# Two sets' w_out_c products run beside the last pair's chain in phase 1 of a hybrid convolution and RWKV-7 step

## The chip, the cores and the metric

The kernel runs on one core of a Trainium2 chip. The metric is the device time of one execution in microseconds; it was timed in three runs, and one further execution was profiled. TensorE (PE) multiplies, with its weight loads counted apart (PEld), VectorE (DVE) and ScalarE (ACT) do the elementwise work, GpSimd (POOL) some of it, and SyncE (SP) issues nearly all DMAs from one queue, in order.

## The reference, cut to what matters

```python
def _layer(x, conv_buf, h_last, S0, norm_g, w_in, conv_w, ...):
    h = _rmsnorm(x, norm_g)
    p = jnp.einsum('bsd,dn->bsn', h, w_in)
    p_conv, p_rwkv, p_gate = _split(p, [N_CONV_COLS, N_RWKV_COLS, 2 * D_MODEL])
    xin, bg, cg, zc = _split(p_conv, CONV_SIZES)
    u = cg * xin
    ...
    y_c = bg * conv * jax.nn.silu(zc)
    ...
    S_fin, ys = _rwkv7_scan(S0, r_h, k_h, v_h, decay.reshape(hs), kk, a_h)
    ...
    y_r = ((yn + bonus) * jax.nn.silu(zr.astype(jnp.float32))).astype(x.dtype)
    gc, gr = _split(p_gate, [D_MODEL, D_MODEL])
    pc = jnp.einsum('bsc,cd->bsd', y_c, w_out_c)
    pr = jnp.einsum('bsc,cd->bsd', y_r, w_out_r)
    m = jax.nn.sigmoid(gc) * pc + jax.nn.sigmoid(gr) * pr
    out = jnp.einsum('bsd,de->bse', m, w_o)
    return x + out, new_conv, h[:, -1], S_fin.astype(S0.dtype)
```

The width D is 1024. The prompt has 2048 tokens; beside it 8 sequences of 4 tokens each continue from a stored state. A final RMSNorm closes the step. All is float32.

## The kernel before

**Sets, pairs, blocks.** The prompt is cut into 4 sets of 512 tokens; the last set (`LAST`) also carries the 32 tokens of the 8 sequences. A block is one projection of 128 output columns over a set: 8 input tiles, three float32r matmuls each (high weights by high input, low by high, high by low), so 24 matmuls of up to 512 columns (`proj`, into one of three PSUM banks called ip). Weights are split into high and low parts once (ACT copy, DVE subtraction, from wraw into whl, 4 buffers each), stored to a scratch in HBM, and loaded from there by the later sets.

**Phase 1.** The main stream runs all input projections, set by set, with the split input in XH and XL. The conv branch's result yc, the gates' tanh gc and gr, and the RWKV branch's result yr go to HBM. Beside the main stream run side jobs (`Side`), one chain of them for each of the 8 head pairs of a set, 32 in all, numbered 0 to 31: keys, solve, merge and load (`begin_pair`), then the chain over 8 chunks (`rwkv_chain`), the 8 sequences (`rwkv_sequences`, last set only) and the group norm with its output (`rwkv_out`), all three started by `run_pair`. A chain step is three small products that wait for each other through DVE and ACT: pa (state by AR), pb (us by the inverse Xbd), pb (SV by BKt, which gives the new state S). A side job gets a stretch of the main stream (`over`, from the fractions in `CUTS`; the unit is three matmuls of 512 columns, 8 to a block), and a clock model (`Clock`) decides between which matmuls each of its steps is put. The scheduler that builds the program moves a few more instructions. The last pair of the last set has 13 own blocks in the main stream; pair 30's chain, sequences and group norm run beside them. Pair 31's run after the main stream's end (`run_pair(*before, 8.0, True)`, `finish_sides`).

**Phase 3.** For each set in turn: a merge stage of 16 blocks (8 by w_out_c with yc in XH and XL, 8 by w_out_r with yr in RH and RL, in turn), where DVE and ACT evacuate with the gates (gt) into MH and ML; then an output stage, 192 matmuls with w_o (240 for the last set) into PSUM banks called po, the residual and the norm. `load_y` brings yc and yr of the next set in during the output stage. Phase 3's tiles take over the SBUF of phase 1's, so their first writers wait for the last users of that memory.

Names in the trace: all compute instructions are issued by one helper, line 117, and all SP DMAs by line 168 (121 and 172 in the changed kernel), so tiles tell the work: ip projections, po output products, pa and pb the chain, pt every other small product.

Of the kernel before, what the change touches and what calls it, by code (L numbers as in the profile page):

```python
# [16 lines left out]
P = 128  # L17
# [7 lines left out]
SIDES = {"first": 8.0, "late": 14.0, "keys": 30.0, "solve": 30.0, "merge": 8.0, "load": 8.0, "samp": 20.0, "out": 12.0, "prep": 10.0, "y": 4.0, "chain": 45.0, "zero": 1.0}  # L25
# [6 lines left out]
        "end": (0.4, 0.1, 0.4, 0.2, 0.4, 0.6, 0.6)}  # L32
WAHEAD = 4

BACKLOG, URGENT = 1800.0, ("chain", "merge", "load", "samp", "prep")
# [140 lines left out]
def hybrid_kernel(tc, x_prompt, x_sample, state_conv, state_shift, state_rwkv, norm_g, w_in, conv_w,  # L176
# [955 lines left out]
    def rwkv_sequences(th, p, o):  # L1132
# [4 lines left out]
        s0 = wraw_p.tile([64, NS, 2, 64], F32, name="wraw")  # L1137
# [106 lines left out]

    EDGE = 3
# [4 lines left out]
    for th in range(NSETS):  # L1250
        for p in range(NB):
# [9 lines left out]
            else:  # L1261
                plan.append((th, whole(bl), p, None))
# [15 lines left out]
    for th in range(NSETS):  # L1278
        for nm, b in MERGE:
            wsrc = w_out_c if nm == "c" else w_out_r  # L1280
            keep(("o" + nm, th, b), wsrc[0][:, b * P:(b + 1) * P])
# [3 lines left out]
    def main_stream(parts):  # L1285
        for x, c0, c1 in parts:
            need(*(job.get(("prep", x.key[1], hf)) for hf in range(2) if (c1 > HN if hf else c0 < HN)))
            yield from x.part(c0, c1)

    def load_y(th, nm):  # L1290
# [5 lines left out]
        def load(b, j):  # L1296
            raw = (wraw_p if th == 0 else o2).tile([P, 1024], F32, name="wraw" if th == 0 else "yraw")[:, 0:nt]
# [91 lines left out]
    for th, hv, p, nx in plan:  # L1389
# [11 lines left out]
        if nx is not None:  # L1401
            e = EDGE / 2 * NB
# [3 lines left out]
    run_pair(*before, 8.0, True)  # L1406
    Side(load_y(0, "c"), "y").over(0, 1)
# [128 lines left out]
```

## Time and profile before

| | |
|---|---|
| runs timed | 3239.68, 3247.93, 3248.16 us; median 3247.93 us |
| profiled execution | 3239.32 us, span 3237.6 us |
| PE busy | 3109.5 us (96%) |
| DVE, ACT, POOL busy | 1999.7 (62%), 1243.0 (38%), 308.7 us (10%) |
| mean granted TensorE clock | 0.987 |
| HBM read and written | 447.90 and 155.17 MB |
| chain that ended last | PE 67%, DVE 20%, ACT 5%, issue 5%, DMA 2% |

A busy engine is one with an instruction in it; TensorE's matmuls are pipelined, so the time of one is longer than the distance to the next. The chain that ended last is followed back from the last instruction to what released each step. Times in rows are from the span's start.

### The profile page before, as it was taken

What the parts mean: (1) busy time and instruction counts of PE and PEld (TensorE: products, weight loads), DVE (VectorE), ACT (ScalarE), POOL (GpSimd) and SP (SyncE); (2) the same over time, 40 slices, a digit from 0 to 9 for tenths busy, and PEclk for the clock granted to TensorE, in tenths of its full rate; (3) what the DMA queues carried; (4) which work ended last, traced back from release to release, by engine and by line L of the source; (5) the groups of instructions that cost most, each with busy time, mean ns of one, the idle gap of its engine ahead of it and who ended that gap; (6) DMA issues with size and microseconds to landing.
All of it is one profiled execution on the core that took longest, in us unless ns stands there. A gap on an engine that the chain in (4) does not pass through costs nothing.

```text
span 3237.6 us, 54951 instructions
## 1 busy us (share of the span) xinstructions
PE 3109.5 (96%) x21234; PEld 2585.9 (80%) x21234; DVE 1999.7 (62%) x5703; ACT 1243.0 (38%) x2580; POOL 308.7 (10%) x517
## 2 busy tenths in 40 slices
PE   7999999999999999999999999999999969999998
PEld 6777777877777778777777899888898847788897
DVE  5687777776666657666666676666777745433332
ACT  5454544444334443443433344443444422211201
POOL 2011111110000111110001010100100000000000
PEclk9999999999999999999999999999999979999999
DMA  7786667644444444444444444434433339988773
GB/s 265 256 269 210 223 221 222 213 158 143 152 161 157 157 155 173 155 159 149 158 157 157 145 159 140 133 135 136 139 130 132 122 126 320 351 307 312 265 257 119
DMA packets 233308, 606.66 MB, mean 187 GB/s; under 512 B 32906, under 2 KB 136451, under 8 KB 179286
## 3 DMA queue, kind: packets, MB, share of 16 engines
q1 hardware_dynamic: 232902, 602.61, 54.4%
q8 instruction: 168, 2.75, 0.3%
q14 instruction: 94, 0.77, 0.1%
q0 software_dynamic: 144, 0.52, 0.0%
HBM read 447.90 MB, written 155.17 MB: 186 GB/s over the span
## 4 chain that ended last, share of the span: by engine, by line
PE 67%; DVE 20%; ACT 5%; issue 5%; DMA 2%; POOL 1%; SPq 0%; ACTq 0%; DVEq 0%; POOLq 0%
PE ip L117 48%; PE pt L117 10%; PE po L117 6%; DVE X L117 3%; DVE tt L117 3%; PE pb L117 3%; DVE tmp L117 2%; ACT tmp L117 2%; DVE Mi L117 2%; DVE whl L117 1%; DVE us L117 1%; DVE S L117 1%; PE pa L117 1%; ACT Xbd L117 1%; DVE GM L117 1%
## 5 line engine op out<-in xcount | busy, mean ns | idle before, releaser
L117 PE MATMUL ip<-XH,whl 128*128 128x512 f32 (+3 forms) x7408 | 2053.4, 356 | 6.6 <-DVE whl L117 1.9
L117 PEld LDWEIGHTS ip<-XH,whl 128*128 128x128 f32 x7408 | 1287.3, 190 | 183.2 <-issue 28.4
L117 PE MATMUL ip<-XL,whl 128*128 128x512 f32 (+3 forms) x3704 | 1316.1, 355 | 2.6 <-POOL XL L117 2.6
L117 PEld LDWEIGHTS ip<-XL,whl 128*128 128x128 f32 x3704 | 702.6, 190 | 80.4 <-issue 6.2
L117 DVE TENSOR_TENSOR X<-X,tt 128x60 f32<-128x60 f32 (+24 forms) x992 | 211.4, 213 | 27.4
L117 DVE TENSOR_TENSOR tt<-Mi,X 128x60 f32<-128x60 f32 (+24 forms) x992 | 209.8, 212 | 28.0
L117 DVE SCALAR_TENSOR_TENSOR S<-pb,pe,sp 64x64 f32<-64x64 f32 x512 | 143.6, 281 | 101.7 <-PE pb L117 95.5
L117 ACT ACTIVATE sp<-S,pe 128x128 f32<-128x128 f32 x256 | 99.5, 399 | 258.2 <-DVE S L117 254.9
L117 ACT ACTIVATE tmp<-ip,vec 128x512 f32<-128x512 f32 (+2 forms) x174 | 103.1, 593 | 231.4 <-PE ip L117 230.0
L117 ACT COPY SV<-pb 64x64 f32<-64x64 f32 x256 | 53.3, 208 | 330.2 <-DVE SV L117 326.3
L117 PE MATMUL ip<-RH,whl 128*128 128x512 f32 (+2 forms) x640 | 170.3, 355 | 4.9 <-ACT RH L117 4.9
L117 PE MATMUL po<-whl,MH 128*128 128x512 f32 x544 | 170.7, 394 | 1.2 <-ACT whl L117 1.1
L117 DVE TENSOR_TENSOR whl<-wraw,whl 128x1024 fp32r<-128x1024 f32 x105 | 134.2, 1279 | 53.3 <-ACT whl L117 52.8
L117 DVE SCALAR_TENSOR_TENSOR gt<-gt,ip 128x512 f32<-128x512 f32 (+1 forms) x80 | 46.9, 586 | 169.3 <-PE ip L117 167.1
L117 DVE TENSOR_TENSOR us<-pa,P 64x64 f32<-64x64 f32 x512 | 110.1, 215 | 57.5 <-PE pa L117 38.4
L117 ACT CAST whl<-wraw 128x1024 fp32r<-128x1024 f32 x105 | 109.5, 1044 | 60.6 <-DMA wraw<-in_w_out_r_dram 25.5
L117 PEld LDWEIGHTS pb<-us,Xbd 128*128 128x128 f32 x512 | 86.4, 190 | 57.6 <-PE ip L117 19.7
L117 PEld LDWEIGHTS ip<-RH,whl 128*128 128x128 f32 x640 | 112.8, 189 | 23.7 <-issue 4.0
L117 PEld LDWEIGHTS pb<-SV,BKt 128*128 128x128 f32 x512 | 85.3, 190 | 57.4 <-ACT SV L117 48.7
L117 PE MATMUL pb<-SV,BKt 128*128 128x128 f32 x512 | 108.1, 293 | 18.6 <-ACT SV L117 18.2
L117 PEld LDWEIGHTS po<-whl,MH 128*128 128x128 f32 x544 | 102.1, 188 | 25.6 <-ACT whl L117 1.6
L117 DVE TENSOR_TENSOR GM<-pt,mask_p 128x512 f32<-128x512 f32 x128 | 82.4, 685 | 61.4 <-PE pt L117 61.4
(489 smaller groups left out, 3940.5 us busy)
## 6 DMA issues: line engine op xcount, KB each, us to landing
wraw<-in_w_in_dram SPq DMA_DIRECT2D x81, 512.0 KB
whl<-w_k SPq DMA_DIRECT2D x24, 1024.0 KB
whl<-w_r SPq DMA_DIRECT2D x24, 1024.0 KB
whl<-w_v SPq DMA_DIRECT2D x24, 1024.0 KB
whl<-w_z SPq DMA_DIRECT2D x24, 1024.0 KB
whl<-w_xin SPq DMA_DIRECT2D x24, 1024.0 KB
whl<-w_cg SPq DMA_DIRECT2D x24, 1024.0 KB
whl<-w_zc SPq DMA_DIRECT2D x24, 1024.0 KB
```

The source lines that it names most:

```text
L117: r = f(*a, **k)
```

## The change

The w_out_c blocks of sets 0 and 1 (`PRE`) are appended to the main stream of the last pair of phase 1, behind its 13 own blocks: 16 blocks, the first three and last three of each set in halves of 256 columns. Their input yc is loaded into the freed buffers of the even pairs (AR0, Xbd0, GM0) and split into XH and XL by half sets (`load_first`), when the last block that reads that half is through. `merge_first` loads gc, forms (gc + 1) times the product, and stores it over gc in HBM. At the end yr of set 1 is loaded the same way. Pair 31's chain, sequences and group norm get stretches of that longer main stream (`TAIL`), pair 30's jobs new fractions (`CUTS["end"]`, of a total that is 238.5 in place of 110.5 units). Phase 3 begins with set 1, whose w_out_r blocks (`merge_second`) read XH and XL, then takes set 0 with w_out_r blocks alone, then sets 2 and 3 as before. gt has 6 buffers in place of 4.

```diff
 CUTS = {"most": (0.7, 0.0, 0.0, 0.34, 0.7, 0.95, 0.95), "last": (0.6, 0.3, 0.68, 0.4, 0.7, 0.97, 0.9),
-        "end": (0.4, 0.1, 0.4, 0.2, 0.4, 0.6, 0.6)}
+        "end": (0.2,0.03,0.22,0.1,0.25,0.32,0.28)}
+
+TAIL = (0.32,0.52,0.32,0.52,0.65)
+PRE = (0, 1)
+FIRST = PRE[-1]
 WAHEAD = 4
...
-        s0 = wraw_p.tile([64, NS, 2, 64], F32, name="wraw")
+        if end_(th, p):
+            s0 = GMB[(th * NB + p + 1) % 2].rearrange("p a b c d -> p (a b c d)")[0:64, 0:NS * P].rearrange(
+                "v (j h k) -> v j h k", h=2, k=64)
+        else:
+            s0 = wraw_p.tile([64, NS, 2, 64], F32, name="wraw")
...
+    def merge_first(th, b):
+
+
+        def begin():
+            o["g"] = tmp.tile([P, TW], F32, name="tmp")
+            SP.dma_start(out=o["g"][:, 0:NT], in_=gc_d[th][b])
+        def evac(c0, c1, ps):
+            g = o["g"][:, c0:c1]
+            V.scalar_tensor_tensor(out=g, in0=g, scalar=1.0, in1=ps[:, 0:c1 - c0], op0=ALU.add, op1=ALU.mult)
+        def end():
+            SP.store(gc_d[th][b], o["g"][:, 0:NT])
+        return Block(("oc", th, b), w_out_c[0][:, b * P:(b + 1) * P], evac, begin, end)
...
+    def load_first(nm, th, hf):
+        cs = slice(hf * HN, (hf + 1) * HN)
+        raws = []
+        for q in range(NB // KG):
+            raws.append(ring[len(turn) % len(ring)])
+            turn.append(q)
+            for i in range(KG // 2):
+                SP.dma_start(out=raws[q][:, 2 * i:2 * i + 2, :],
+                             in_=(yc_d if nm == "c" else yr_d)[th][q * KG // 2 + i][:, :, cs])
+        yield "free", raws
+        for q, raw in enumerate(raws):
+            split(XH[:, q * KG:(q + 1) * KG, cs], XL[:, q * KG:(q + 1) * KG, cs], raw)
+            yield 1
...
-                plan.append((th, whole(bl), p, None))
+                own = whole(bl[:-EDGE]) + by_halves(bl[-EDGE:])
+                hv = list(own)
+                for t in PRE:
+                    cm = [merge_first(t, b) for b in range(NB)]
+                    hv += by_halves(cm[:EDGE]) + whole(cm[EDGE:-EDGE]) + by_halves(cm[-EDGE:])
+                plan.append((th, hv, p, length(own)))
...
+    ORDER3 = list(PRE[::-1]) + [th for th in range(NSETS) if th not in PRE]
+    for th in ORDER3:
+        for nm, b in [x for x in MERGE if x[0] == "r" or th not in PRE]:
...
-            need(*(job.get(("prep", x.key[1], hf)) for hf in range(2) if (c1 > HN if hf else c0 < HN)))
+            kind = (x.key[0], x.key[1]) if x.key[0] in ("oc", "or") else ("prep", x.key[1])
+            need(*(job.get((*kind, hf)) for hf in range(2) if (c1 > HN if hf else c0 < HN)))
             yield from x.part(c0, c1)
...
-            raw = (wraw_p if th == 0 else o2).tile([P, 1024], F32, name="wraw" if th == 0 else "yraw")[:, 0:nt]
+            raw = o2.tile([P, 1024], F32, name="yraw")[:, 0:nt]
...
     def run_pair(th, p, total, end):
 
         k = th * NB + p
-        f = [total * x for x in CUTS["end" if end else "most" if th < LAST else "last"]]
+        c1, s0, s1, _, _, _, o1 = CUTS["end" if end else "most" if th < LAST else "last"]
+        c0, c1, s0, s1, o1 = (total * x for x in (TAIL if end_(th, p) else (0.0, c1, s0, s1, o1)))
         after = [prior("merge", k), prior("load", k), prior("out", k - 1)]
-        job["chain", k] = Side(rwkv_chain(th, p, outs[k]), "chain", after).over(0, f[0])
+        job["chain", k] = Side(rwkv_chain(th, p, outs[k]), "chain", after).over(c0, c1)
         done = [job["chain", k]]
         if th == LAST:
-            job["samp", k] = Side(rwkv_sequences(th, p, outs[k]), "samp", after).over(f[1], f[2])
+            job["samp", k] = Side(rwkv_sequences(th, p, outs[k]), "samp", after).over(s0, s1)
             done.append(job["samp", k])
-        job["out", k] = Side(rwkv_out(th, p, outs[k]), "out", done).over(max(f[0], f[2]), f[6])
+        job["out", k] = Side(rwkv_out(th, p, outs[k]), "close" if end_(th, p) else "out", done).over(max(c1, s1), o1)
...
+        e = EDGE / 2 * NB
+        if end_(th, p):
+            run_pair(th, p, total, True)
+            f = [nx] + [nx + NB * NB * (i + 1) for i in range(len(PRE))]
+            behind, start = job["out", LAST * NB + p - 1], nx - 6 * NB
+            for (nm, t), at, back in zip([("c", t) for t in PRE] + [("r", FIRST)], f, [EDGE * NB * (NTT[th] - HN) / NT] + [e] * len(PRE)):
+                for hf, x in enumerate((at - back, at)):
+                    behind = job["o" + nm, t, hf] = Side(load_first(nm, t, hf), "prep", [behind], gate=x + 0.01).over(start, x)
+                    start = x + 0.02
+        elif nx is not None:
             job["prep", th + 1, 0] = Side(prep(th + 1, 0), "prep", gate=nx - e + 0.01).over(nx - 2 * e, nx)
             job["prep", th + 1, 1] = Side(prep(th + 1, 1), "prep", gate=nx + 0.01).over(nx - e, nx + e)
         drive(main_stream(hv))
-    run_pair(*before, 8.0, True)
-    Side(load_y(0, "c"), "y").over(0, 1)
     finish_sides()
...
+    def merge_second(b):
+        def begin():
+            for nm, src in (("r", gr_d), ("c", gc_d)):
+                o[nm] = o2.tile([P, WM], F32, name="gt", bufs=6)
+                SP.dma_start(out=o[nm][:, 0:NT], in_=src[FIRST][b])
+        def evac(c0, c1, ps):
+            merged(FIRST, b, o["r"], o["c"], c0, c1, ps)
+        return Block(("or", FIRST, b), w_out_r[0][:, b * P:(b + 1) * P], evac, begin)
...
-            g = gt[(nm, b)] = o2.tile([P, WM], F32, name="gt", bufs=4)
+            g = gt[(nm, b)] = o2.tile([P, WM], F32, name="gt", bufs=6)
-            if nm == "r":
-                need(job.get(("y", th)))
+            if nm == "c" and th in PRE:
+                continue
...
-    for th in range(NSETS):
-        if th == 0:
-            job["y", 0] = Side(load_y(0, "r"), "y").over(0, NB)
-        drive(merge_stage(th))
+    for th, then in zip(ORDER3, ORDER3[1:] + [None]):
+        if th == FIRST:
+            rm = [merge_second(b) for b in range(NB)]
+            drive(main_stream(by_halves(rm[:EDGE]) + whole(rm[EDGE:])))
+        else:
+            drive(merge_stage(th))
...
-        if th < LAST:
-            Side(in_turn(load_y(th + 1, "c"), load_y(th + 1, "r")), "y").over(0, n)
+        if then is not None:
+            Side(in_turn(*(load_y(then, nm) for nm in "cr" if nm == "r" or then not in PRE)), "y").over(0, n)
```

TensorE, pair 31's last chain steps, sequences and group norm, in the kernel before (pa and pb are chain steps, wraw holds the sequences' old states, Yc the chunk outputs that the group norm transposes):

```order
L117 MATMUL pa<-S_478,AR_203 128x128
L117 MATMUL pb<-us,Xbd_209 128x64
L117 MATMUL pb<-SV,BKt 128x128
L117 MATMUL pt<-ident,S_478 128x128
L117 MATMUL pt<-ident,wraw 128x64 x8
L117 MATMUL pt<-tmp,AR_203 128x512 x2
L117 MATMUL pt<-us_28944,Xbd_209 128x64
L117 MATMUL pt<-tmp,BKt 64x512 x2
L117 MATMUL pt<-ident,tmp 64x128 x8
L117 MATMUL pt<-SV,GM_207 64x64 x18
L117 MATMUL pt<-ident,Yc 128x128 x4
L117 MATMUL pt<-ident,Yc 64x128
```

TensorE, a chain step of pair 31 in the changed kernel, in set 0's w_out_c blocks:

```order
L121 MATMUL ip<-XH,whl 128x512 x2
L121 MATMUL pa<-S_478,AR_203 128x128
L121 MATMUL ip<-XL,whl 128x512
L121 MATMUL ip<-XH,whl 128x512 x2
L121 MATMUL ip<-XL,whl 128x512
L121 MATMUL ip<-XH,whl 128x512 x2
L121 MATMUL pb<-us,Xbd_209 128x64
L121 MATMUL ip<-XL,whl 128x512
L121 MATMUL ip<-XH,whl 128x512 x2
L121 MATMUL ip<-XL,whl 128x512
L121 MATMUL ip<-XH,whl 128x512 x2
L121 MATMUL pb<-SV,BKt 128x128
```

The products that stood one behind the other now have ip matmuls of w_out_c blocks between them.

SP's queue at the seam of the phases in the kernel before (yr from tmp is pair 31's result, gt are the first gates of phase 3):

```order
L168 DMA wraw<-yr_1_89 128x512
L168 DMA yr_3_103<-tmp 128x544
L168 DMA wraw<-yr_2_90 128x512 x2
L168 DMA wraw<-yr_3_91 128x512
L168 DMA gt<-gc_0_104 128x512
L168 DMA gt<-gc_1_105 128x512
L168 DMA gt<-gr_0_136 128x512
```

SP's queue at the same seam in the changed kernel:

```order
L172 DMA gc_5_117<-tmp 128x512
L172 DMA wraw<-in_w_out_r_dram 128x8x128
L172 DMA gc_6_118<-tmp 128x512
L172 DMA wraw<-in_w_out_r_dram 128x8x128
L172 DMA gc_7_119<-tmp 128x512
L172 DMA w_or_377<-whl 128x2048
L172 DMA gt<-gr_0_144 128x512
L172 DMA gt<-gc_0_112 128x512
L172 DMA gt<-gr_1_145 128x512
L172 DMA gt<-gc_1_113 128x512
```

The first gt loads now stand behind the stores of set 1's last merged gates (gc from tmp) and between the weights of w_out_r; the store of yr stands 16 rows ahead of them.

## Rows read from the trace of the kernel before

**Rows 1.** The page, part 2: tenths of busy time or clock in 40 slices.
```profile
PEclk9999999999999999999999999999999979999999
DMA  7786667644444444444444444434433339988773
```

**Rows 2.** Windows: length, busy us (instructions) of PE, PEld, DVE, ACT, POOL; clock; DMA share; GB/s.
```profile
2609.40:2682.80 73.40, 44.91 (x189) 28.64 (x185) 37.94 (x87) 21.86 (x50) 5.58 (x4) 0.67 0.39 130
2682.80:2756.30 73.50, 73.48 (x316) 59.38 (x317) 36.20 (x43) 19.42 (x22) 0.00 (x0) 1.00 0.98 340
2756.30:2890.00 133.70, 130.70 (x560) 104.30 (x559) 51.69 (x90) 25.82 (x45) 2.23 (x4) 1.00 0.88 328
```

**Rows 3.** Timeline of PE, 2608 to 2673: start, length, instructions, [idle before, releaser].
```profile
2608.24 1.26 PE L117 MATMUL pt<-SV,GM 64*64 64x64 f32 x36
...
2614.24 2.05 PE L117 MATMUL ip<-XH,whl 128*128 128x512 f32 x4
...
2672.40 1.19 PE L117 MATMUL ip<-RH,whl 128*128 128x512 f32 x2 [3.62 <-ACT RH L117]
```

**Rows 4.** The chain of waits at the seam of the phases: start, length, what.
```profile
2673.16 1.69 POOL tmp L117
2674.87 2.17 DMA yr<-tmp
...
2677.11 4.94 DMA gt<-gc
...
2682.82 73.51 PE ip L117 x315
2756.33 0.70 PE po L117 x3
```

**Rows 5.** Waits of PE, 2608 to 2683: us in total, times, longest.
```profile
PE pt L117 <- DVE Yc L117: 7.9, 1, 7.9
PE ip L117 <- ACT RH L117: 4.3, 2, 3.6
```

**Rows 6.** Groups of PE by form, 2000 to 2500, six pairs: count, busy us, mean ns.
```profile
L117 PE MATMUL pb<-SV,BKt 128*128 128x128 f32 x96 | 19.5, 285 | 0.6 <-ACT SV L117 0.4
L117 PE MATMUL pa<-S,AR 128*128 128x128 f32 x96 | 19.5, 285 | 1.0 <-DVE S L117 0.8
...
L117 PE MATMUL pb<-us,Xbd 128*128 128x64 f32 x96 | 16.8, 256 | 3.7 <-DVE us L117 3.3
...
L117 PE MATMUL pt<-SV,GM 128*64 128x64 f32 x216 | 7.6, 225 | 0.0
L117 PE MATMUL pt<-SV,GM 64*64 64x64 f32 x216 | 7.6, 221 | 0.0
...
L117 PE MATMUL pt<-tmp,AR 64*128 64x512 f32 x24 | 6.8, 641 | 0.0
L117 PE MATMUL pt<-ident,tmp 128*64 128x128 f32 x48 | 6.6, 273 | 0.0
```

**Rows 7.** Timeline of PE, 2597 to 2598: first matmul of 256 and of 288 columns.
```profile
2597.01 0.40 PE L117 MATMUL ip<-XH,whl 128*128 128x256 f32 x2
...
2598.07 0.42 PE L117 MATMUL ip<-XH,whl 128*128 128x288 f32 x2
```

**Rows 8.** Windows, six pairs of the last set under full cover.
```profile
2000.00:2500.00 500.00, 487.38 (x4373) 446.27 (x4373) 353.38 (x1162) 207.24 (x506) 42.13 (x67) 1.00 0.40 134
```

**Rows 9.** DMA issues of the whole run: count, KB each.
```profile
whl<-w_oc SPq DMA_DIRECT2D x24, 1024.0 KB
...
gt<-gc SPq DMA_DIRECT2D x24, 256.0 KB
...
wraw<-in_w_out_c_dram SPq DMA_DIRECT2D x8, 512.0 KB
```

**Rows 10.** Timeline of SP, 2809 to 2810, second merge stage: a weight load's issue.
```profile
2809.28 0.38 SPq L168 DMA_DIRECT2D whl<-w_oc  x1
```

**Rows 11.** Timeline of PE, 2816: the matmul that waited for that load.
```profile
2816.29 0.70 PE L117 MATMUL ip<-XH,whl 128*128 128x512 f32 x2 [1.15 <-DMA whl<-w_oc]
```

More of the change, by code (lines that the diff above doesn't have):

```diff
@@ L24 @@
 HN = NT // 2
-SIDES = {"first": 8.0, "late": 14.0, "keys": 30.0, "solve": 30.0, "merge": 8.0, "load": 8.0, "samp": 20.0, "out": 12.0, "prep": 10.0, "y": 4.0, "chain": 45.0, "zero": 1.0}
+SIDES = {"first": 8.0, "late": 14.0, "keys": 30.0, "solve": 30.0, "merge": 8.0, "close": 12.0, "load": 8.0, "samp": 20.0, "out": 12.0, "prep": 10.0, "y": 4.0, "chain": 45.0, "zero": 1.0}
 W = {"sq": 1.0, "norm": 1.0, "lora": 2.0, "one": 1.0, "scan": 2.0, "exp": 2.0, "key": 1.0, "bones": 1.5,
@@ L31 @@
 CUTS = {"most": (0.7, 0.0, 0.0, 0.34, 0.7, 0.95, 0.95), "last": (0.6, 0.3, 0.68, 0.4, 0.7, 0.97, 0.9),
-        "end": (0.4, 0.1, 0.4, 0.2, 0.4, 0.6, 0.6)}
+        "end": (0.2,0.03,0.22,0.1,0.25,0.32,0.28)}
+TAIL = (0.32,0.52,0.32,0.52,0.65)
+PRE = (0, 1)
+FIRST = PRE[-1]
 WAHEAD = 4
-BACKLOG, URGENT = 1800.0, ("chain", "merge", "load", "samp", "prep")
+BACKLOG, URGENT = 1800.0, ("chain", "merge", "close", "load", "samp", "prep")
 class Clock:
@@ L1243, in length @@
         return sum((c1 - c0) / NT * NB for _, c0, c1 in parts)
+    def merge_first(th, b):
+        o = {}
+        def begin():
[7 more added lines that the diff above has]
+        return Block(("oc", th, b), w_out_c[0][:, b * P:(b + 1) * P], evac, begin, end)
+    ring, turn = [], []
+    def load_first(nm, th, hf):
+        cs = slice(hf * HN, (hf + 1) * HN)
+        if not ring:
+            ring.extend(t[:, o:o + KG * HN].rearrange("p (k t) -> p k t", t=HN) for t, o in (
+                (ARB[0].rearrange("p a b c -> p (a b c)"), 0), (XB[0].rearrange("p a b -> p (a b)"), 0),
+                (GMB[0].rearrange("p a b c d -> p (a b c d)"), NS * P)))
+        raws = []
[9 more added lines that the diff above has]
+            yield 1
     EDGE = 3
@@ L1420, in hybrid_kernel, with merged @@
     RH, RL, MH, ML = (o1.tile([P, NB, WM], F32R, name=nm) for nm in ("RH", "RL", "MH", "ML"))
+    def merged(th, b, g, gc, c0, c1, ps):
+        V.scalar_tensor_tensor(out=g[:, c0:c1], in0=g[:, c0:c1], scalar=1.0, in1=ps[:, 0:c1 - c0], op0=ALU.add, op1=ALU.mult)
+        V.tensor_tensor(out=g[:, c0:c1], in0=gc[:, c0:c1], in1=g[:, c0:c1], op=ALU.add)
+        A.activation(out=MH[:, b, c0:c1], in_=g[:, c0:c1], func=AF.Identity, scale=0.5)
+        V.scalar_tensor_tensor(out=ML[:, b, c0:c1], in0=g[:, c0:c1], scalar=0.5, in1=MH[:, b, c0:c1].bitcast(F32),
+                               op0=ALU.mult, op1=ALU.subtract)
+    def merge_second(b):
+        o = {}
+        def begin():
[5 more added lines that the diff above has]
+        return Block(("or", FIRST, b), w_out_r[0][:, b * P:(b + 1) * P], evac, begin)
     def merge_stage(th):
@@ L1432, in merge_stage @@
                 ps = yield from proj(w, (XH, XL) if nm == "c" else (RH, RL), c0, c1 - c0)
-                V.scalar_tensor_tensor(out=g[:, c0:c1], in0=g[:, c0:c1], scalar=1.0, in1=ps[:, 0:c1 - c0],
-                                       op0=ALU.add, op1=ALU.mult)
-                if nm == "r":
-                    V.tensor_tensor(out=g[:, c0:c1], in0=gt[("c", b)][:, c0:c1], in1=g[:, c0:c1], op=ALU.add)
-                    A.activation(out=MH[:, b, c0:c1], in_=g[:, c0:c1], func=AF.Identity, scale=0.5)
-                    V.scalar_tensor_tensor(out=ML[:, b, c0:c1], in0=g[:, c0:c1], scalar=0.5,
-                                           in1=MH[:, b, c0:c1].bitcast(F32), op0=ALU.mult, op1=ALU.subtract)
+                if nm == "c":
+                    V.scalar_tensor_tensor(out=g[:, c0:c1], in0=g[:, c0:c1], scalar=1.0, in1=ps[:, 0:c1 - c0],
+                                           op0=ALU.add, op1=ALU.mult)
+                else:
+                    merged(th, b, g, gt[("c", b)], c0, c1, ps)
     def rows_of(th):
```

5 lines of the change are left out of this document (1 added, 4 removed).

## Prediction

> **What bounds the kernel now.** The page is read first: TensorE is busy in every slice, at nearly its full clock, but for a dent just before the last stage, where both its clock and the DMA share fall, and after which the DMA rises to nine tenths and more [rows 1]. So up to the dent TensorE's own work sets the time, the dent is where something else does, and behind it TensorE and the DMA are both near their limits. The windows by stretch give the dent its bounds: in 73.4 us TensorE ran only 189 instructions, was busy 44.91 us and was granted 0.67 of its clock, a mix of its two levels; the 73.5 us behind it hold 316 instructions without a gap [rows 2]. TensorE's own list tells what it is. The last phase 1 block ends at 2608.24 with nothing left to run beside pair 31's chain, sequences and group norm; two blocks of the first merge stage fill its middle; then, until the first RH matmul at 2672.40, only the chain's and the sequences' small products run [rows 3]. The chain of waits closes the seam: the group norm's last POOL step, the store of yr (2.17 us), then the load of gc (4.94 us), and from 2682.82 TensorE alone [rows 4]. The waits of that stretch name VectorE and ScalarE steps between dependent products, not one resource [rows 5]. It is latency, and latency can be covered by other matmuls.
>
> **What the dent costs.** From 2608.24 [rows 3] to the first output product at 2756.33 [rows 4] are 148.1 us. The work in it that has to be done is the first merge stage, 16 blocks of 24 matmuls at 512 columns. Their pitch is 73.50 / 316 = 0.2326 us [rows 2], so 384 x 0.2326 = 89.3 us. The other 58.8 us belong to pair 31's tail.
>
> **What the tail costs when it is covered.** Its products still take TensorE time. From six pairs under full cover [rows 6]: the chain's three groups (19.5 + 19.5 + 16.8) / 6 = 9.3 us a pair; the two SV,GM forms 15.2 / 6 = 2.5; the tmp,AR products 6.8 / 6 = 1.1, and the mirrored BKt products, taken as equal, 1.1; the transposes of the new states 6.6 / 6 = 1.1. Some 16 instructions are left (old states, us2, S, Yc), at that row's 6.6 / 48 = 0.14 us another 2.2. Together 17.3; I take **17 us**, a little less, since the rows overlap the neighbouring matmuls. Bounds 15 and 20. So 58.8 - 17 = **41.8 us** can go at most.
>
> **What the change does, part by part.**
> - It moves sets 0 and 1's 16 w_out_c blocks ahead of the seam, as cover. Their matmuls are the same ones: at 0.2326 us they cost 89.3 us there and save 89.3 us behind (two merge stages run 8 blocks instead of 16). Zero, as long as they run at that pitch. The listing shows chain steps separated by three to six matmuls where they stood alone.
> - It halves 12 of these blocks, and 3 of the second half-stage. A run of nine 256-column matmuls took 2598.07 - 2597.01 = 1.06 us, 0.118 each [rows 7]; two halves cost 0.236 against 0.2326, 0.003 more: 15 x 24 x 0.003 = **+1.1 us**.
> - It spreads the chain, sequences and group norm over the covered 107 us (89.3 + 17 + 1). Six such pairs left TensorE idle for 500 - 487.4 = 12.6 us in 500 [rows 8], 2.5%: **+2.8 us**.
> - It moves the evacuation and the splits with the blocks. VectorE was busy 353 of 500 us in those pairs [rows 8], and the dent's own VectorE work was already there, so the added steps (one a block, and the splits that phase 3 loses) hide behind matmuls. Zero; if VectorE fell behind, the three ip banks would fill and it would be the next to be late.
> - It makes a new seam. A g buffer lies where a gt buffer will, so the first gt load waits for the last store of gc. By the old seam that is 2.17 + 4.94 us [rows 4], plus about 1 us of evacuation: 8.1 us. TensorE meanwhile has three half blocks of r in three banks, 3 x 24 x 0.118 = 8.5 us. Nearly covered; I take **+2 us**. Bounds 0 (cover holds) and 8 (no cover).
> - It adds DMA: for 16 blocks a store of gc and a second load, 32 x 256 KB = 8.4 MB [rows 9], and puts loads of 1 KB rows on SP's one queue, among stores that wait. Queued behind SP's wait for a split are the next weights. A 1024 KB weight load issued at 2809.28 was awaited until 2816.29: 7.0 us under load [rows 9 to 11]. At the edge between the two sets a buffer comes free three half blocks (8.5 us) before its successor is needed. It fits by 1.5 us.
> - DMA as a whole, in the units of [rows 9], from the last own block to the end of the first output stage: w_out_c raw, stored and reloaded 3 + 8 + 8, gc 8, yc and yr 4, w_out_r raw and stored 4 + 8, gt 4, w_o raw and stored 4 + 8, x 2, y 2, yr and first weights of the next set 5: 68 x 1.05 = 71 MB in 107 + 8 blocks of 5.58 us + 192 x 0.2326 us = 196 us, 363 GB/s. That is over the 340 GB/s that a 98% busy DMA moved [rows 2]. But counted alike, the old first merge and output stages ask for (w_out 7 + 16, yr 1, gt 4, w_o 4 + 8, x 2, y 2, next set 7) 51 x 1.05 = 54 MB in 134 us, 400 GB/s, and TensorE still stood idle for only 133.7 - 130.7 = 3.0 us behind the first merge stage [rows 2], since stores and prefetches spill into the lighter stage that follows. I take **+4 us**. Bounds 0 and 25 (the added 8.4 MB at 340 GB/s with nothing to hide it).
>
> A page speaks against the last step. The Trainium skill, page "DMA: Bandwidth & Descriptors", section "Bandwidth", has traffic between HBM and SBUF bound at about 358 GB/s a core (and 425 measured for one large transfer with the neighbour core idle); by 358 the 71 MB would take 198 us, 2 us more than TensorE needs, so the term would be 2. The same section asks for transfers of 1 MiB and more, which the new 256 KB loads break. The trace does not bear a loss out: the stretch of [rows 2] that reached 340 GB/s had 256 KB and 512 KB loads between its large ones [rows 9].
>
> **The sum.** -41.8 + 1.1 + 2.8 + 2 + 4 = **-31.9 us**. The profiled execution took 3239.32 us (span 3237.6 and 1.7 around it): 3207.4. Three runs were timed at 3239.68 to 3248.16, median 3247.93, so the profiled one lies 8.6 below the median. Which end the changed kernel's median takes is not told by the trace; I add half, 4.3, and say **3212 us**.
>
> **Rivals.**
> 1. *DMA becomes the bound in the new stretch.* If nothing spills, 71 MB at 340 GB/s take 209 us against 196: 13 us in place of 4, sum -22.9, 3216 to 3225 us. For it: 98% share in the old first merge stage, and now such traffic lasts longer. Against it: 3.0 us of idle TensorE where the old demand was larger [rows 2]. Chance 0.13.
> 2. *The queue loses rate, and the kernel is slower.* The new loads are of 1 KB rows, mixed with stores, and SP's queue holds weights behind waits for splits. If the stretch moves only 290 GB/s, 71 MB take 245 us: 49 us of stall, -41.8 + 1.1 + 2.8 + 2 + 49 = +13, about 3252 to 3261 us. It decides from where the stall exceeds 36 us, which is 71 / 232 = 306 GB/s. For it: at 88% share the DMA moved 328 GB/s, 373 for a full share, at 98% only 340, 347 for a full share [rows 2], so the rate does fall with the mix. Against it: that fall is 7%, and this one would have to be 12% more. Chance 0.06.
> 3. *The tail is not fully covered.* The sequences or the group norm end late, block SP (the last yr store stands before the second w_out_r weight and the last yr load), and the seam shows again with 8 us and some 8 us of waits more: -41.8 + 1.1 + 11 + 8 + 4 = -18, 3221 to 3230 us. For it: the schedule comes from a planner's costs, and phase 1 has short waits of this kind. Against it: 2.5% idle in six pairs [rows 8]. Chance 0.09.
> That the change does not do what it says is ruled out by the listing. The forecast keeps 0.72: 3199 to 3216 us.
>
> **Range and chances.** Low end: 15 us of tail and only the 2.8 us of waits give -39.9 on the profiled time, 3199, and a little for what no row shows: 3197. High end: seam 7, DMA 25 give -6, 3233, so 3234; that takes in rivals 1 and 3. A measurement of this kernel tells about 0.3%, 10 us, from no change, so faster means under 3238 us. The forecast and rivals 1 and 3 all lie there but for a tail of each: faster 0.87, same 0.07, slower 0.06.
>
> **What would show it.** Right: no stretch before the seam with a granted clock near 0.67; chain steps 3 us or more apart with ip matmuls between their products; TensorE waits of 10 us or less from the last own block to the first output product; DMA share over 0.9 from the first moved block on; two merge stages of 45 us. Wrong: TensorE waiting for whl, XH or gt for tens of microseconds (rivals 1 and 2), Yc or us waits of several microseconds each (rival 3). A saving beyond 42 us would mean that the tail's products cost less than 15 us or that something else moved.

## The result, and the profile after

The changed kernel takes **3208.49 us** (median of four runs, 3207.27 to 3210.94), beside 3245.69 us for the kernel before in the same session (3239.68 to 3248.16). The ratio is 0.9889, 95% interval 0.9877 to 0.9901: 1.1% faster. The profiled execution took 3209.42 us (span 3207.7), 29.9 less than the profiled one of before. The forecast was 3212 us in a range of 3197 to 3234. Two executions in a slower state, 3361.9 us of the kernel with one set and spare banks and 3392.2 us of the kernel before, both at a granted clock below 0.85, are left out of every median and ratio here.

The page of the changed kernel, part 2, as in [rows 1]:

```profile
PEclk9999999999999999999999999999999999999999
DMA  8786666644444444444444444343443469988863
```

The slice with 7 tenths of the clock is gone, and so is the dip of the DMA ahead of the last stage. The windows that answer to [rows 2]: from the first moved blocks to the seam, from there to the first output product, and on to 2890.

```profile
2609.40:2732.30 122.90, 116.65 (x898) 109.71 (x897) 57.68 (x110) 31.94 (x51) 5.29 (x4) 1.00 0.90 310
2732.30:2770.40 38.10, 38.08 (x193) 32.71 (x194) 20.55 (x34) 10.92 (x16) 0.00 (x0) 0.96 1.04 387
2770.40:2890.00 119.60, 116.15 (x499) 93.00 (x498) 50.37 (x87) 27.15 (x51) 3.26 (x4) 1.00 0.87 333
```

Where 73.4 us held 189 TensorE instructions at 0.67 of the clock, 122.9 us now hold 898 at 1.00. TensorE's waits from 2609 to 2770 (us in total, times, longest), in place of [rows 5]:

```profile
PE ip L121 <- DVE gt L121: 3.5, 1, 3.5
PE ip L121 <- DVE tmp L121: 1.2, 1, 1.2
PE pb L121 <- DVE us L121: 0.6, 1, 0.6
PE pt L121 <- DVE SV L121: 0.5, 1, 0.5
PE ip L121 <- DVE nw L121: 0.4, 1, 0.4
```

The tail, that is pair 31's chain, sequences and group norm, had left TensorE waiting for up to 7.9 us at a time; it costs 1.5 us of waits now (us, SV, nw). The longest wait is a new one, for gt, at the new seam. TensorE's timeline (start, length, what, idle before and its releaser): a mark that is used below, a wait in pair 31's inverse, a step of its chain, the seam, and the first output product.

```profile
2567.82 0.27 PE L121 MATMUL pt<-ident,S 128*128 128x128 f32 x1
...
2593.50 0.77 PE L121 MATMUL pt<-Xbd,sq 128*128 128x128 f32 x2 [1.96 <-DVE Xbd L121]
...
2618.68 0.38 PE L121 MATMUL pa<-S,AR 128*128 128x128 f32 x2
...
2620.76 0.39 PE L121 MATMUL pb<-us,Xbd 128*128 128x64 f32 x2
...
2622.34 0.38 PE L121 MATMUL pb<-SV,BKt 128*128 128x128 f32 x2
...
2732.32 0.50 PE L121 MATMUL ip<-XH,whl 128*128 128x256 f32 x2 [3.46 <-DVE gt L121]
...
2770.36 0.62 PE L121 MATMUL po<-whl,MH 128*128 128x512 f32 x2
```

**Where the time went.** The first of these rows, the transposition of pair 30's final state, is a mark that every kernel here has. Before, it stood at 2566.62:

```profile
2566.62 0.33 PE L117 MATMUL pt<-ident,S 128*128 128x128 f32 x1
```

From there to the first output product [rows 4] are 189.7 us before, and 190.2 if the 1152 columns are added that the old order has ahead of the mark and the new one behind it. After, it is 202.5 us with eight blocks more (24 x 0.2326 = 5.58 us each, 44.6 together): 157.9 like for like, **32.3 us less**. From the first output product to the end of the span are 481.3 us before, 436.6 without those eight blocks, and 437.3 after. So the whole gain is in that one stretch. The medians differ by 37.2. Where the other 4.9 us of that lie the profiled executions don't show; runs of one kernel scatter by more, and over the 14 kernels profiled here the mark alone stands anywhere from 2562.05 to 2570.07.

The stretch can be cut further, in windows of 4 us from the mark on: TensorE's idle time; its busy time multiplied by what is missing to the full clock; and what is left, its work at full clock. Before, these are 30.8, 13.7 and 145.7 us, after 8.4, 6.1 and 143.4. The gain is 22.4 us of waiting, 7.6 of clock and 2.3 of work. (The three parts add up to the stretch by construction, and each is read from one execution of a kernel; the work of the kernels that cover the tail, all with the same products, differs by up to 2 us.) The table has this for each kernel, with the ratio to the runs of before on the same chip; stretch and rest are without the eight blocks, wherever the kernel has them.

| kernel | ratio, 95% interval | median us | stretch | idle | clock | work | rest |
|---|---|---|---|---|---|---|---|
| before | | | 190.2 | 30.8 | 13.7 | 145.7 | 436.6 |
| change | 0.9889, 0.9877 to 0.9901 | 3208.49 | 157.9 | 8.4 | 6.1 | 143.4 | 437.3 |
| before without tail | 0.9858, 0.9844 to 0.9871 | 3195.17 | 146.4 | 12.2 | 5.2 | 129.0 | 435.2 |
| change without tail | 0.9868, 0.9852 to 0.9883 | 3197.98 | 144.6 | 11.8 | 2.8 | 130.0 | 437.4 |
| tail behind the moved blocks | 1.0036, 1.0023 to 1.0050 | 3253.16 | 205.9 | 44.1 | 15.5 | 146.3 | 435.5 |
| one set | 0.9916, 0.9902 to 0.9929 | 3212.41 | 159.1 | 13.3 | 2.8 | 143.0 | 443.1 |
| one set, spare banks | 0.9914, 0.9898 to 0.9930 | 3213.99 | 157.9 | 9.1 | 5.8 | 143.0 | 443.2 |
| no gc store | 0.9864, 0.9850 to 0.9878 | 3198.86 | 152.3 | 4.8 | 4.6 | 142.9 | 437.1 |
| second gc stores from SP | 0.9939, 0.9925 to 0.9952 | 3221.71 | 172.1 | 21.0 | 8.5 | 142.6 | 439.7 |
| second gc stores from POOL | 0.9918, 0.9905 to 0.9930 | 3218.31 | 164.7 | 12.9 | 8.1 | 143.7 | 438.6 |
| no kept w_out_c | 0.9889, 0.9874 to 0.9905 | 3208.03 | 157.4 | 7.0 | 6.2 | 144.2 | 438.5 |
| spare banks | 0.9880, 0.9866 to 0.9894 | 3203.10 | 151.1 | 4.7 | 3.2 | 143.2 | 439.4 |
| spare banks, no kept w_out_c | 0.9885, 0.9871 to 0.9898 | 3206.72 | 151.0 | 3.4 | 3.2 | 144.4 | 438.6 |
| spare banks, no stall | 0.9857, 0.9840 to 0.9873 | 3195.51 | 144.9 | 0.7 | 0.0 | 144.2 | 438.2 |

### The profile page after: what moved, and what is told of

Read it like the earlier page. It is cut to its first block, busy times and chain, and to the rows that moved or that the text cites. A ratio compares the mean times of both kernels' runs of the same rounds, so it can differ in the third digit from the quotient of the medians.

```text
span 3207.7 us, 55738 instructions
## 1 busy us (share of the span) xinstructions
PE 3102.1 (97%) x21594; PEld 2603.2 (81%) x21594; DVE 1999.0 (62%) x5712; ACT 1241.4 (39%) x2571; POOL 309.9 (10%) x517
## 5 line engine op out<-in xcount | busy, mean ns | idle before, releaser
L121 PE MATMUL ip<-XH,whl 128*128 128x512 f32 (+3 forms) x7776 | 2107.3, 351 | 10.2 <-DVE gt L121 3.5
L121 PEld LDWEIGHTS ip<-XH,whl 128*128 128x128 f32 x7776 | 1341.8, 190 | 184.2 <-issue 30.4
L121 PE MATMUL ip<-XL,whl 128*128 128x512 f32 (+3 forms) x3888 | 1362.9, 351 | 2.6 <-POOL XL L121 2.6
L121 PEld LDWEIGHTS ip<-XL,whl 128*128 128x128 f32 x3888 | 738.5, 190 | 77.4 <-issue 6.2
L121 DVE SCALAR_TENSOR_TENSOR S<-pb,pe,sp 64x64 f32<-64x64 f32 x512 | 143.7, 281 | 100.7 <-PE pb L121 94.6
L121 PE MATMUL ip<-RH,whl 128*128 128x512 f32 (+2 forms) x512 | 128.5, 341 | 1.1 <-DMA whl<-w_or 0.6
L121 PE MATMUL pb<-us,Xbd 128*128 128x64 f32 x512 | 90.1, 258 | 22.5 <-DVE us L121 21.9
L121 ACT COPY Xbd<-Xo 32x256 f32<-32x256 f32 x128 | 88.2, 689 | 61.2 <-DVE Xo L121 59.1
```

Source lines behind the costliest of these rows:

```text
L121: r = f(*a, **k)
```

## The experiments

### Is the gain the cover of the tail?

Both kernels without pair 31's chain, sequences and group norm; the edit is the same in each:

```diff
 def rwkv_chain(th, p, o):
+    if end_(th, p):
+        yield 0.0
+        for h in range(2):
+            SP.dma_start(out=new_rwkv_p[0, 0, 2 * p + h], in_=St[p][HS[h], HS[h]])
+        return
...
 # rwkv_sequences, behind the load of s0: s0 written back, return
 # rwkv_out: yr stored from bv, return
```

> The kernel before without the same three parts of pair 31 (S, the loaded states and bv written as they are). Theory: the tail cost 58.8 us there, so about 3246 - 58.8 = 3187, 3182 to 3193 us, and the change without the tail lies within 5 us of it: with no tail to cover, moving the blocks gains nothing. Rival (a part of the gain is not the tail's cover): the change without its tail is 10 us or more faster than this.

> The change without pair 31's chain, sequences and group norm: S and the loaded states are written back as they are, and bv stands in place of yr. Theory: under cover the tail costs TensorE 17 us and 2.8 us of waits, so 3208.5 - 19.8 = about 3189, 3184 to 3194 us. Rival (the tail is partly bare in the change, by 10 us or more): 3178 us or less. Rival (its products slip into gaps and cost nothing): 3203 us or more.

Without the tail the two kernels agree: ratios 0.9858 and 0.9868 with overlapping intervals, stretches of 146.4 and 144.6 us. Moving the blocks is worth 32.3 us with the tail and 1.8 without, so the gain is the tail's cover. But both came out slower than expected, by 8 and 9 us and above their ranges, and the waits say why. Before without the tail, TensorE's waits to 2756:

```profile
PE ip L117 <- ACT XH L117: 7.1, 2, 6.7
PE ip L117 <- ACT whl L117: 2.4, 1, 2.4
```

and the change without it:

```profile
PE ip L121 <- DVE tmp L121: 5.1, 4, 2.7
PE ip L121 <- DVE gt L121: 4.5, 1, 4.5
```

Without the tail, TensorE reaches the inputs of the merge before they are loaded and split, and 12 us of idle time take its place in both, with 3 to 5 us of lower clock behind. The work is the cleaner measure: the tail's products cost 143.4 - 130.0 = 13.4 us in the change, good to 1 or 2 us by the scatter of that column.

Next, the order and place of the blocks kept, and the cover taken away:

```diff
-            run_pair(th, p, total, True)
...
         drive(main_stream(hv))
+    run_pair(*before, 8.0, True)
...
+    def behind_moved(x):
+        V.scalar_tensor_tensor(out=x, in0=newest[-1], scalar=0.0, in1=x, op0=ALU.mult, op1=ALU.add)
```

> The change with pair 31's chain and sequences made to wait for the last moved block (one element of S and of s0 is added to with zero times an element of the last merged gc), so that all 16 moved blocks stand where the change put them, but the tail has only the three first halves of r, 8.5 us, beside it. Theory (the gain is the cover of the tail): the tail shows again. Before, it cost 58.8 us of the stretch against 17 + 2.8 covered; with 8.5 us of matmuls beside it instead of two blocks, 3208.5 + 58.8 - 19.8 = about 3247, 3238 to 3255 us. Rival (the gain is in phase 3: other order of the sets, six gt buffers, the merge stages of two sets halved): 3208 to 3218 us.

It took 3253.16 us, slower than before by 0.36% (0.23 to 0.50), and the stretch 205.9: the rival falls, and the rest behind the first output product is what it was. The windows of this kernel show the dent back, now behind the moved blocks:

```profile
2720.00:2740.00 20.00, 11.11 (x30) 7.38 (x30) 5.71 (x24) 4.42 (x14) 0.00 (x0) 0.50 0.29 80
2740.00:2760.00 20.00, 10.74 (x63) 5.91 (x63) 10.48 (x19) 1.18 (x5) 0.00 (x0) 0.50 0.06 15
2760.00:2780.00 20.00, 2.06 (x8) 1.64 (x9) 4.50 (x14) 3.66 (x7) 5.21 (x4) 0.50 0.25 84
```

TensorE runs at 1.2 GHz throughout (clock 0.50), and the tail ends in an 11.2 us wait for gt: 5.5 us of it are the store of yr and the load of gt, one behind the other (2773.75 to 2779.24), the rest the last steps of the group norm.

### Is half the cover enough?

```diff
-PRE = (0, 1)
+PRE = (0,)
```

with the fractions of `CUTS["end"]` and `TAIL` times 238.5/174.5.

> The change with only set 0's eight blocks moved, the table's fractions scaled to the shorter stretch (238.5/174.5), so that the tail stands at the same blocks. Cover falls from 107 to 62 us, the added gc traffic from 8.4 to 4.2 MB. Theory (what matters is that each latency of the tail has matmuls beside it, and 62 us are about the tail's own 58.8 + 17 of length): most of the gain stays, 3208 to 3222 us, with waits of the chain and the sequences of up to 13 us where the cover is too short. Rival (DMA costs time in the new stretch, and half of it would be saved): 3196 to 3205 us. Second rival (62 us is too short and the tail's end stands bare): 3222 to 3235 us.

Nearly: 0.9916, and the stretch is only 1.2 us longer, so 62 us of matmuls cover the tail almost as well as 107 do. The waits up to 2890 that the change does not have, or has shorter:

```profile
PE ip L121 <- DVE gt L121: 8.6, 1, 8.6
PE ip L121 <- ACT XH L121: 5.1, 2, 2.6
```

The wait for gt at the seam is 5.1 us longer; that the stretch grew by 1.2 only is due to the clock, of which 3.3 us less were lost than in the change (the section on the 2 us wait has the place). The rest is 5.8 us more than the change's: set 1's w_out_c blocks are in phase 3 again, and their input XH is split late. The same kernel with the spare PSUM banks that are described below:

> One set moved instead of two, and the same five spare banks. Theory: with one set the seam waited 8.6 us for gt, which the spare banks cover: 8 to 11 us less than the one-set kernel's 3212.4, 3201 to 3205 us, no slower than the change with spare banks, with 4.2 MB less to move each way. Rival (with one set the tail's end and the loads of set 1 come late, and other waits take the place): 3207 to 3212 us.

The wait for gt went, but the time did not follow (3213.99 us, ratio 0.9914, 0.9898 to 0.9930): waits of 3.0 us for tmp, 1.4 for SV and 1.4 for Yc stand in the stretch, 3.0 us more of clock are lost in it, and XH costs 6.2 us behind it. The rival held in kind, and the time came out above its range too. So the second set seems to pay by what it takes out of phase 3 (5.8 us of rest) more than as cover; no run parts the two further.

### Is the new stretch bound by the DMA?

Without the stores of the merged gc, and with each of them made twice:

```diff
-            SP.store(gc_d[th][b], o["g"][:, 0:NT])
+            pass
```

```diff
             SP.store(gc_d[th][b], o["g"][:, 0:NT])
+            SP.store(gx_d[th][b], o["g"][:, 0:NT])
```

> The change without the 16 stores of the merged gc (4.2 MB, so the gates are read back unmerged; that part of the output is left out). Theory (the seam waits for the landing of the last gc store, 6.3 us after its issue, and DMA costs nothing else): the first gt load goes out right behind the last evacuation, 5 to 6 us earlier, the 3.5 us wait at the seam goes, and with it some 1.5 us at the lower clock behind it: 3 to 6 us less than the change's 3207 to 3208, 3201 to 3205 us. Rival (DMA is the bound in the new stretch): 4.2 MB less at 340 GB/s are 12 us on top, 3196 us or less.

> The change with each merged gc stored a second time, to a scratch tensor that nothing reads: 16 stores of 256 KB, 4.2 MB more in the new stretch. Theory (the DMA has room, since stores and prefetches spill into the next stage; only the queue ahead of the first gt load grows): 0 to 4 us more than the change, 3207 to 3212 us, all of it at the seam. Rival (DMA is the bound there): 12 us more, 3218 us or more.

The first came out near its theory, the second did not. Without the stores the wait for gt is gone, the ratio is 0.9864 and the stretch 5.6 us shorter, within the 3 to 6 expected of the seam; the median, 3198.86, is below the expected range by 2 us, less than its own runs scatter (3192.39 to 3202.29). With second stores the stretch is **14.2 us longer**, as the rival said, but not at the seam. (The profiled execution, 3228.23 us, is the slowest of its five; by the medians the stores cost 13.2 us.) Its waits ahead of the first output product:

```profile
PE ip L121 <- ACT whl L121: 9.6, 1, 9.6
PE ip L121 <- DVE tmp L121: 7.4, 1, 7.4
```

To part the bytes from the queue, the same second stores were issued by POOL:

```diff
+            nc.gpsimd.dma_start(out=gx_d[th][b], in_=o["g"][:, 0:NT])
```

> The same 4.2 MB of second stores as in the run with more stores (15 us over the change), but issued by POOL, so that SP's one queue and its list of waiting stores are as in the change. Theory A (the bytes cost the time: the stretch is at the DMA's limit): 12 to 15 us over the change again, 3218 to 3222 us. Theory B (the second stores on SP's in-order queue pushed waits in front of the loads of gc and the weights, and the bytes fit): 0 to 5 us over the change, 3207 to 3212 us. Something between would divide the 15 us.

Something between: 0.9918, the stretch 6.8 us longer, with 4.8 us of wait for gt, 2.4 for tmp, 1.6 for SV and 0.8 for whl. By the stretches about half of the 14.2 us come with the bytes from either queue (4.2 MB take 12.3 us at 340 GB/s, so nearly half of that is hidden), and the other half only when SP's one queue issues them. That division is not firm: by the medians the two kernels cost 13.2 and 9.8 us, and their intervals overlap (0.9925 to 0.9952, 0.9905 to 0.9930). That the added bytes cost time holds by either measure. Then bytes were taken away: w_out_c is loaded raw and split at each use, never stored.

```diff
+            if kind[0] == "oc":
+                order.append((key, src, None, False))
+                return
```

> The change itself with w_out_c loaded raw at each use, without the spare banks. Theory (the last gc store took 6.3 us to land because the DMA was 97% busy): with 12.6 MB less in the stretch it lands in 2 to 3 us as the yr store did before, the first gt comes in time, the seam's 3.5 us shrink to under 1, and the other late loads go too: 3201 to 3205 us. Rival (the landing is slow for another reason, as that the store is small rows or stands behind others on the queue): the seam keeps 3 us or more, 3205 to 3210 us.

> The spare-banks kernel with w_out_c's blocks loaded raw (512 KB) and split at each of their four uses, instead of split once, stored and reloaded (1024 KB each): in the moved stretch 8.4 MB loaded in place of 4.2 + 8.4 + 8.4 MB moved, 12.6 MB less, against 24 more splits (1.23 us of VectorE and a copy on ScalarE each). Theory (the waits left are late loads, and VectorE and ScalarE have room): the waits for tmp and whl behind 2600, some 5 us, go, 3198 to 3202 us. Rival (the splits come late, or the waits left are not the DMA's): 3203 us or more.

Both rivals held, so less traffic gained nothing: 3208.03 us (0.9889, 0.9874 to 0.9905) is no gain on the change, 3206.72 us (0.9885, 0.9871 to 0.9898) none on the spare-banks kernel that follows below. The windows of the change and of the kernel without kept weights, ahead of the wait at the seam in both:

```profile
2609.00:2725.00 116.00, 113.20 (x871) 106.53 (x871) 55.51 (x108) 31.18 (x51) 5.29 (x4) 1.00 0.89 308
```

```profile
2609.00:2725.00 116.00, 115.43 (x882) 108.27 (x881) 64.96 (x115) 40.05 (x58) 6.15 (x4) 1.00 0.74 234
```

The DMA went from 308 to 234 GB/s (8.6 MB less in 116 us). TensorE's wait of 1.2 us for tmp is gone, but the one for gt is not, the work came out 0.8 us higher, and the whole stretch is 0.5 us shorter, less than can be told apart. More traffic cost time, less traffic saved none that shows: by these runs the change stands close to the point where the DMA begins to bind, and not beyond it.

### What is the new seam?

The change's SP (issues) and VectorE around the seam:

```profile
2721.42 0.62 SPq L172 DMA_DIRECT2D gc<-tmp  x1
2722.14 0.38 SPq L172 DMA_DIRECT2D w_or<-whl  x1
2727.77 0.32 SPq L172 DMA_DIRECT2D gt<-gr  x1
```

```profile
2727.97 0.10 DVE L121 MEMSET fs<- 128x10 f32 x2 [2.14 <-DMA gc<-tmp]
...
2731.84 0.42 DVE L121 SCALAR_TENSOR_TENSOR gt<-gt,ip 128x256 f32<-128x256 f32 x1 [2.56 <-DMA gt<-gr]
```

From the issue of the last gc store to its landing are 6.3 us (SP goes on at 2727.77), and to the first use of gt 10.4. That this store is what the wait hangs on is shown by the kernel without the gc stores, where the wait is gone. The kernel without kept weights has the store issued at 2718.84 and the same two rows of VectorE at 2723.91 and 2729.17, 10.3 us again, and the wait:

```profile
PE ip L121 <- DVE gt L121: 3.6, 1, 3.6
```

So how busy the DMA was in the 116 us ahead does not set it. At the seam itself, though, the DMA was hardly less busy there than in the change; from the issue of the store to the first use of gt, the change and this kernel:

```profile
2721.42:2731.84 10.42, 7.44 (x63) 7.16 (x61) 3.65 (x5) 2.10 (x2) 0.77 (x1) 1.00 1.02 348
```

```profile
2718.84:2729.17 10.33, 7.29 (x62) 7.09 (x61) 2.34 (x4) 0.74 (x1) 0.77 (x1) 1.00 0.92 326
```

Stores of w_or, 1 MB each, stand about the last gc store in the queue in both. Whether it is they that make store and load slow was not tried, and stays open. The wait can be covered, though:

```diff
-        ps = ps_ip.tile([P, 512], F32, name="ip")
+        ps = spare.pop(0).tile([P, 512], F32, name="po") if spare else ps_ip.tile([P, 512], F32, name="ip")
...
             rm = [merge_second(b) for b in range(NB)]
+            spare.extend([ps_o] * 5)
```

> The change with the first five half blocks of r written to the five output banks of PSUM, which stand empty until the first output stage, so that TensorE has eight half blocks and then whole ones ahead of it, 17 us and more, before it needs the first gt. Theory (the seam's 3.5 us are a wait for a buffer and a load, not for work): the wait goes and with it the lower clock behind it: 3 to 5 us less than the change, 3202 to 3205 us. Rival (weights or loads are late next, the stretch is bound by the DMA): no gain, 3206 to 3209 us, and the wait stands at whl or at po.

As expected: 3203.10 us (0.9880, 0.9866 to 0.9894, which overlaps the change's interval, so that the stretch carries the verdict). TensorE's waits from 2568 to the first output product hold no gt any more. The stretch is 6.8 us shorter than the change's, 3.7 of it idle time and 2.9 clock. Behind the change's seam the clock was

```profile
2732.00:2736.00 4.00, 3.68 (x20) 3.68 (x21) 2.22 (x6) 0.83 (x2) 0.00 (x0) 0.65 0.97 293
2736.00:2740.00 4.00, 4.00 (x34) 4.00 (x33) 2.98 (x7) 1.66 (x3) 0.00 (x0) 0.92 1.03 431
```

which is 3.68 x 0.35 + 4 x 0.08 = 1.6 us lost, 5.1 with the wait.

### What does a 2 us wait cost?

The change's windows around the wait for Xbd at 2593.50 (the clock is the third number from the end):

```profile
2590.00:2594.00 4.00, 2.04 (x39) 1.83 (x31) 0.82 (x3) 0.99 (x3) 2.69 (x2) 0.91 0.45 168
2594.00:2598.00 4.00, 4.00 (x47) 3.78 (x45) 0.58 (x2) 0.38 (x1) 0.00 (x0) 0.50 1.01 278
2598.00:2602.00 4.00, 4.00 (x23) 3.32 (x21) 1.71 (x4) 0.70 (x2) 0.00 (x0) 0.50 0.08 21
2602.00:2606.00 4.00, 4.00 (x30) 3.60 (x30) 2.15 (x5) 1.25 (x2) 0.00 (x0) 0.81 0.10 18
```

and those of before, where the same wait took 1.99 us:

```profile
2590.00:2594.00 4.00, 2.01 (x13) 1.78 (x12) 0.91 (x3) 0.48 (x2) 1.68 (x2) 0.89 0.73 293
2594.00:2598.00 4.00, 4.00 (x26) 4.00 (x26) 1.92 (x3) 1.04 (x1) 0.00 (x0) 0.68 0.42 172
2598.00:2602.00 4.00, 4.00 (x33) 3.85 (x33) 0.11 (x1) 0.79 (x2) 0.00 (x0) 1.00 0.50 203
```

Before, the clock came back within 4 us, in the change after 8 to 10. Busy time by missing clock is 2.01 x 0.11 + 4 x 0.32 = 1.5 us before and 2.04 x 0.09 + 4 x (0.50 + 0.50 + 0.19) = 4.9 in the change: 3.4 us that no step of the prediction had. Here the change has the first small products of pair 31's tail (36 SV,GM products of 64x64 and the first chain steps), which stood behind the own blocks before. The last run takes the wait away on top of the spare banks; the additions of the identity in pair 31's inverse leave VectorE, where they queue behind a step that waits for POOL.

```diff
-            V.tensor_tensor(out=M, in0=M, in1=ident, op=ALU.add)
+            T.matmul(pt[:, P:2 * P], lhsT=ident, rhs=M, start=True, stop=False)
+            T.matmul(pt[:, P:2 * P], lhsT=ident, rhs=ident, start=False, stop=True)
+            A.copy(M, pt[:, P:2 * P])
```

and the same for the two products that follow.

> The spare-banks kernel (3203.1) with the three additions of the identity in pair 31's inverse taken from VectorE, where they queue behind a convolution step that waits 4 us for POOL, and made by a small accumulating product of the identity and a ScalarE copy instead. In the change TensorE waits 1.96 us for the first of them at 2591.5 and then runs at half its clock until about 2603, 8 to 10 us, where before it was at half for about 4 us only. Theory (the short stall is what brings the clock down, and a lower clock over 8 to 10 us costs 4 to 5 us): the wait and the dip both go: 4 to 6 us less, 3197 to 3199 us, and the granted clock stays at 1.0 from 2590 to 2606. Rival (the clock falls because of the many small products there, whatever waits): only the wait goes, 3200 to 3202 us, and the dip stays. Second rival (the wait moves to ScalarE's copies): 3202 to 3205 us.

It did, and more: **3195.51 us**, 0.9857 (0.9840 to 0.9873), the fastest of the kernels that compute everything, faster than the change by intervals that don't meet. The stretch is 6.2 us shorter than with the spare banks alone (idle 0.7 in place of 4.7, no clock lost), nothing but work is left in it, and the clock stays up although the small products are still there:

```profile
2590.00:2594.00 4.00, 4.00 (x60) 3.35 (x58) 1.28 (x2) 0.81 (x3) 0.00 (x0) 1.00 0.98 275
2594.00:2598.00 4.00, 4.00 (x41) 3.80 (x37) 2.38 (x5) 2.40 (x4) 0.00 (x0) 1.00 0.72 206
2598.00:2602.00 4.00, 3.93 (x24) 2.78 (x24) 3.54 (x6) 1.29 (x4) 0.00 (x0) 1.00 0.59 198
```

So the wait brings the clock down, and not the small products by themselves. Whether they keep it down longer can be read from the other thirteen kernels, which all have the wait (1.94 to 1.99 us). In the four without these products behind it (before, both kernels without the tail, and the tail behind the moved blocks) the 18 us from the wait's end on lost 1.6 to 1.7 us of clock, counted in windows of 2 us; in eight of the nine with them 3.4 to 5.0; and in the ninth, with one set, only 1.6. The change without the tail, and then the kernel with one set, in the first 8 us from the wait's end:

```profile
2588.35:2592.35 4.00, 4.00 (x22) 3.64 (x23) 1.09 (x3) 0.38 (x1) 0.00 (x0) 0.59 0.98 274
2592.35:2596.35 4.00, 4.00 (x35) 4.00 (x34) 2.27 (x4) 2.38 (x3) 0.00 (x0) 1.00 0.31 78
```

```profile
2587.70:2591.70 4.00, 4.00 (x47) 3.77 (x47) 0.58 (x2) 0.38 (x1) 0.00 (x0) 0.60 0.96 272
2591.70:2595.70 4.00, 4.00 (x41) 3.68 (x36) 2.35 (x6) 1.91 (x4) 0.00 (x0) 1.00 0.26 71
```

So a long dip comes only with the small products behind the wait, but not each time; what decides stays open. The same edit in the kernel before was not run.

## Why the prediction was right, step by step

The time, its sign and its mechanism came out: 3208.49 us against 3212, and on the stretch -32.3 us against a sum of -31.9. That the sum is so close is partly chance, since errors of both signs met in it.

- **The bare tail**, 58.8: before had 30.8 us idle and 13.7 of clock, of which the wait in pair 31's inverse has 2.0 and 1.5 in any case, and 145.7 - 129.0 = 16.7 of products: 57.7. Right.
- **The covered tail**, 17 with bounds of 15 and 20, and 2.8 of waits: it cost 13.4 of products and 1.5 of waits (us, SV, nw). This term was mis-sized: it summed the durations of the products' rows [rows 6]; by the work that went with them they cost less than that, and less than the lower bound. The sign of 3 us or more between chain steps came true (4.4 to 15.6 us from pa to pa between 2618 and 2655), but it tells little: in the bare tail of before they stood 3 to 4 us apart as well.
- **The halves**, +1.1: too small to be told apart in any run.
- **The seam**, +2 with bounds of 0 and 8: mis-sized, it cost 5.1. The step carried the 2.17 us of a yr store in an idle dent [rows 4] over to a store in a busy stretch; that landing took 6.3 us, so store and load took 10.4 in place of 7.1, and with the 1 us of evacuation that is past the 8.5 us of three half blocks. And the clock behind a wait had no price.
- **The DMA**, +4 with bounds of 0 and 25: too large. The waits that can be put down to loads are the 1.2 us for tmp, and 3.6 us of waits behind the first output product against 2.9 before. 8.6 MB less saved nothing that shows. By the Trainium skill, page "DMA: Bandwidth & Descriptors", section "Bandwidth", some 358 GB/s bound a core, and 425 were measured for one large transfer with the neighbour core idle. The trace goes above the first, 387 GB/s for the 38 us behind the seam, and in one window of 4 us there it reaches 431.
- **The dip** behind the wait in the inverse, 3.4 us more than before: not in the prediction. The wait stood in the trace of before, and what it costs in clock there, 1.5 us, could be read; what was missed is what the change puts behind it.
- Together 57.7 - 14.9 - 5.1 - 1.2 - 3.4 = 33.1, for the 32.3 measured.
- **The place of the profiled run**, +4.3: not needed. The profiled run of before lies 6.4 us below the median of its runs and that of the change 0.9 above its own.
- **The rivals.** The first, that the DMA becomes the bound, did not come true, but the change is close to it: 4.2 MB more cost 6.8 us of stretch. The second, that the queue makes the kernel slower, did not either, yet it names what a careless edit meets: on SP's own queue the same bytes cost 14.2 us in the profiled execution. The third is refuted by the waits; the last yr store is issued at 2704.96, 27 us before the seam.

## What to carry to other kernels

Latency that stands alone at the end of a stage can be covered by independent matmuls that can be brought there; the gain is the bare time less what its products cost under cover, and half the cover did nearly as well here. Price each wait of TensorE with the clock behind it, above all where small products follow: a wait of 2 us cost 3.5 before and 7 after, clock included. Where a buffer passes from one stage to the next through a store and a load, count both at the landing times of a busy queue, and give TensorE that many microseconds of banks.

## What the runs showed of the hardware

- After a TensorE wait of 1.96 us the granted clock was at its lower level (1.2 GHz) for 8 to 10 us, after one of 1.99 us before for about 4, and with no wait it did not fall, with the same small products in place. In the four kernels with no small products behind the wait the clock lost came to 1.6 to 1.7 us, in eight of nine with them to 3.4 to 5.0, in the ninth to 1.6.
- A store of 256 KB landed 6.3 us after its issue from SP, and 16 of them from POOL's queue took 6.4 us in the median (DMA share 0.93 up to the seam), against 2.17 us for a store of yr in the dent (272 KB, the DMA moving 182 GB/s). By the Trainium skill, page "DMA: Bandwidth & Descriptors", section "Latency and other measured facts", a lighter load on HBM makes the fixed part of a DMA smaller. From before to after the rows agree (182 GB/s in all while the store of yr ran, 348 at the new seam); no run here has a gc store with a lightly loaded DMA at the seam itself.
- In a stretch where the DMA share was 0.90, 4.2 MB more cost 6.8 us of stretch from POOL's queue and 14.2 from SP's (9.8 and 13.2 by the medians), while 8.6 MB less up to the seam saved none that shows.
